# Whole-tile order between readers and writers of PSUM in a recorded program, and one PSUM tile per half for the sums by head

## The chip, the cores and the metric

The kernel runs on one core of one Trainium2 chip. The metric is the device time in microseconds (us) of one execution; the time before is the median of three runs, 963.48 us (959.92 to 965.08).

## The reference

One layer of a hybrid encoder block on 512 tokens of width 1024, in float32. What matters here:

```python
h = rms_norm(x, norm1_g) * (1.0 + sc1) + sh1
xr, yr, q, k, v, gates = jnp.split(h @ w_in, IN_SPLITS, axis=-1)
xr = depthwise_conv(xr, conv_rnn_w, conv_rnn_b, RNN_CONV_LEFT)
# two gates for each of two directions, then two scans
r = sigmoid(einsum('bsnk,dnkj->dbsnj', xb, w_a) + b_a)
i = sigmoid(einsum('bsnk,dnkj->dbsnj', xb, w_i) + b_i)
log_a = -8.0 * r * softplus(-lam)
u = sqrt(-expm1(2.0 * log_a)) * (i * xc)
branch_a = ((h_fwd + h_bwd) * gelu(yr)) @ w_rnn_o
# differential attention, then an RMS norm over each head
o = rms_norm(o, subln_g) * (1.0 - lam_init)
branch_b = o @ w_attn_o
x = x + g1 * ((sigmoid(gate_A) * branch_a + sigmoid(gate_B) * branch_b) @ w_out)
x = x + g2 * (convffn(rms_norm(x, norm2_g) * (1.0 + sc2) + sh2) @ w_down)
return rms_norm(x, final_g)
```

## The kernel before, in words

**Recording and planning.** The kernel's Python code does not issue its instructions at once. A `Recorder` for each engine adds a node to a `Program` (`instruction`, line 203), and `use` (line 182) finds the nodes that it has to come after: a reader comes after the writes that overlap its area of the tile, a writer after the overlapping writes and reads. An area is a box of partitions and columns, so two parts of one tile that do not overlap put no order on each other. Besides, every matmul comes after the last matmul into the same bank (512 columns) of its tile, and a new tile in a buffer comes after all uses of the tile before it.

At the end `order` (line 248) runs through the nodes as a list planner. Each engine has a clock of its own; whenever it is free, it takes the earliest recorded node that is able to run. `cost` (line 226) sets the prices, in a unit of the planner's own: a matmul in FP32R costs its columns plus 32 (544 for 512 columns), one in FP32 four times its columns plus 300 (1324 for 256), a ScalarE activation of 512 columns from PSUM 1581, a new activation table 3080 more. What a matmul releases on another engine is able 360 later. ScalarE ranks a node that needs another table 100 places lower (`PATIENCE`, line 71), but takes it if nothing else is able. The instructions are then emitted in the order of the planned starts, and the tile framework adds the semaphores that this order and the tiles ask for. So the planner decides each engine's queue, and which of two instructions on one tile stands first; how long anything takes on the chip is not its to decide.

**The stages that the change touches.** In the order of time:

- First norm (lines 1019 to 1081): the sum of squares of 512 tokens stands in one PSUM tile `ss1`, written in two halves of 256 columns by FP32 matmuls. ScalarE takes the inverse root of each half into `rstd` (line 1040), then splits the first weight block (`whi`, line 1041); VectorE refines the roots (`newton`, line 635).
- Input convolution: `xrw` is a PSUM tile of two banks for two blocks of 128 channels; `conv_rnn` (line 775) reads each bank by itself.
- Gates (`gates`, line 1143): for each of 8 blocks and 2 directions a PSUM tile `pri` of two banks, [128, 2, 512]. Three matmuls fill bank 0, then three bank 1; then the task `gate` has ScalarE read bank 0 (sigmoid into `r`) and bank 1 (sigmoid into `i`). In between TensorE works through the queue of dense products (`run`, line 583).
- Recurrence (`decays`, `scans`): exponentials, roots and gelus on ScalarE, scans on VectorE.
- Attention: for each head and query block `softmax` (line 1260), four transposes into the tile `pt` (`transposed`, line 1291), two ScalarE copies and two VectorE subtractions that each read half of it, and `product` (line 1316).
- Norm by head: `head_sums` (line 1352) adds 16 matmuls of 256 columns for one half of the tokens into `ssh`, `head_rows` (line 1364) reads that half on ScalarE and VectorE. `ssh` is one tile of two banks, a bank for each half, from the pool `psc` with two buffers; `gates`, `softmax` and `pu` (line 1544) use the same two.
- Output product and second norm: `half` (line 1525) fills the PSUM tiles `op6` and `op7` half by half, and a residual step reads each half.

Of the kernel before, what the change touches and what calls it, by code (L numbers as in the profile page):

```python
# [18 lines left out]
P = 128  # L19
# [3 lines left out]
HEADS = 8  # L23
# [144 lines left out]
class Program:  # L168
# [13 lines left out]
    def use(self, view, write, n, after):  # L182
        t = view.base
        p0, p1, c0, c1 = view.area
        after.add(t.node)

        def meets(u):
            return u[1] < p1 and p0 < u[2] and u[3] < c1 and c0 < u[4]

        after.update(u[0] for u in t.writes if meets(u))  # L190
        if write:
            after.update(u[0] for u in t.reads if meets(u))

            def covered(u):
                return p0 <= u[1] and u[2] <= p1 and c0 <= u[3] and u[4] <= c1

            t.reads = [u for u in t.reads if not covered(u)]
            t.writes = [u for u in t.writes if not covered(u)]
            t.writes.append((n, p0, p1, c0, c1))
        else:  # L200
            t.reads.append((n, p0, p1, c0, c1))

    def instruction(self, engine, owner, name, args, kwargs):
        n, after = len(self.nodes), set()
# [171 lines left out]
def build(nc, tc, ctx, a, out):  # L376
    program = Program(nc)
    V, A, G, T = (
        Recorder(program, e, o) for e, o in ((DVE, nc.vector), (ACT, nc.scalar), (POOL, nc.gpsimd), (PEQ, nc.tensor))
    )  # L380
# [18 lines left out]
    def H(name, dt=F32):  # L399
        n = unused.popleft()  # L400
        t = heap.tile([P, S], dt, tag=f"s{n}", name=name)
        slot_of[id(t)] = n, t
        return t

    def free(*tiles):
        for t in tiles:
            if isinstance(t, (list, tuple)):
                free(*t)
            else:
                unused.append(slot_of.pop(id(t))[0])  # L410
# [14 lines left out]
    def bank2(name):  # L425
        return psc.tile([P, 2, S], F32, tag="sc", name=name)
# [11 lines left out]
    def spawn(gen, delay=0):  # L438
        task = [now[0] + delay, gen]
        tasks.append(task)  # L440
        if not delay:
            advance(task)
# [8 lines left out]
    def until(ready):  # L451

        while not ready():
            assert tasks
            tick()
# [13 lines left out]
    def load(src, n):  # L469
        raw = wraw.tile([P, n], F32, tag="raw", name=f"raw{fetched[0]}")  # L470
        sync.dma_start(raw, src)
        return raw
# [110 lines left out]
    def run(n):  # L583

        while n > 0 and finished[0] < limit[0]:
            r = next(st)
            n -= r
            owed[0] += r
            while owed[0] >= 3:
                owed[0] -= 3  # L590
                tick()
# [6 lines left out]
    for k in range(NK):  # L598
        t = H(f"x{k}")
# [4 lines left out]
    def v(name, j=0, n=1):  # L604
        return vec[:, VEC[name][0] + j : VEC[name][0] + j + n]
# [24 lines left out]
    def inverse_rms(ss, n, r, q):  # L630

        A.activation(r, ss, AF.Abs_reciprocal_sqrt, scale=1.0 / n)
        newton(ss, n, r, q)

    def newton(ss, n, r, q):
        V.tensor_tensor(q, r, r, mult)
        V.scalar_tensor_tensor(q, q, -0.5 / n, ss, mult, mult)
        V.scalar_tensor_tensor(r, q, 1.5, r, add, mult)
# [365 lines left out]
    w = load(a["w_xr"][0], 7 * P)  # L1004
# [33 lines left out]
    rstd, q, t = H("rstd1"), H("rstd1q"), H("hf0")  # L1038
# [40 lines left out]
    w = whi, wlo  # L1079
# [8 lines left out]
    for k in range(NK):  # L1088
        parts3 = (0, 0), (1, 0), (0, 1)
        if k + 1 < NK:  # L1090
            n = k + 1
            t = H(f"hf{n}")
# [27 lines left out]
        for n, (i, j, m, f) in enumerate(passes):  # L1120
            T.matmul(
                xr[m][:, f], w[i][:, m * P : (m + 1) * P], h[k][j][:, f], start=k + i + j == 0 and m == 6,
                stop=k == NK - 1 and i == 0 and j == 1,
# [11 lines left out]
        w = following  # L1135
# [142 lines left out]
    def scores(n, head, qt):  # L1278
        until(lambda: len(qk.get(head, ())) == 3)
        qs, kh, kl = qk[head]  # L1280
        sc = bank2(f"sc{head}{qt}")
        f = slice(qt * P, (qt + 1) * P)
        for c in range(2):
            T.matmul(sc[:, c, :], qs[c][:, f], kh[c], start=True, stop=False)
            T.matmul(sc[:, c, :], qs[c][:, f], kl[c], start=False, stop=True)
        tick()
        spawn(softmax(n, head, qt, sc))
        if qt == 3:
            free(qk.pop(head))
# [26 lines left out]
    def product(head, half):  # L1316
        w = wt.pop((head, half))
        until(lambda: len(w) == 3 and (head // 2, 1) in vs)
        if half == 0:
            po[head] = bank1(f"po{head}", "po")  # L1320
        f = slice(half * 256, half * 256 + 256)
        for k in range(4):
            vv = [b[:, k % 2, (head % 2) * P : (head % 2) * P + P] for _, b in vs[head // 2, k // 2]]
            g = slice((k % 2) * 256, (k % 2) * 256 + 256)
            mm3(po[head][:, f], vv, [t[k // 2][:, g] for t in w[:2]], k == 0, k == 3)
        tick(2)
        free(w[:2])
        if half == 0:
            oT[head] = H(f"oT{head}")
        if half == 1 or head == HEADS - 1:  # L1330
            g = f if head == HEADS - 1 else slice(0, S)
            A.copy(oT[head][:, g], po[head][:, g])
        if half == 1:
            if head % 2 == 1:
                free([[t for t, _ in vs[head // 2, i]] for i in range(2)])
# [4 lines left out]
    def square(j, f):  # L1340
        sq = H(f"osq{j}{f.start}")
        sqs = [H(f"osqs{j}{f.start}{i}", F32R) for i in "hl"]
        A.activation(sq[:, f], oT[j][:, f], AF.Square)
        A.copy(sqs[0][:, f], sq[:, f])
        yield 2
        V.scalar_tensor_tensor(sqs[1][:, f], sq[:, f], EPS, sqs[0][:, f].bitcast(F32), add, sub)
        free(sq)
        for g in HALVES:
            if f.start <= g.start and g.stop <= f.stop:
                squares[j, g.start] = sqs  # L1350

    def head_sums(i, js):
        f = HALVES[i]
        for j in js:
            until(lambda: (j, f.start) in squares)
            sqs = squares[j, f.start]
            for c in range(2):
                w = sel[:, 8 * j : 8 * j + 8]
                T.matmul(ssh[:8, i, :256], w, sqs[c][:, f], start=j + c == 0, stop=j + c == HEADS)
            if i or j == HEADS - 1:  # L1360
                free(sqs)
            run(HS[i])

    def head_rows(i):
        f = HALVES[i]
        inverse_rms(ssh[:8, i, :256], P, rh[:8, f], rhq[:8, f])
        yield 3
        A.copy(rhs[0][:8, f], rh[:8, f])
        yield 1
        V.tensor_tensor(rhs[1][:8, f], rh[:8, f], rhs[0][:8, f].bitcast(F32), sub)  # L1370
        rows.append(i)
# [27 lines left out]
    for n in range(len(steps) + LAG + LAGP):  # L1399
        if n < len(steps):  # L1400
            scores(n, *steps[n])
        if n == len(steps) - 2:
            gsub = keep.tile([P, 1], F32, name="gsub")
            V.tensor_scalar(gsub, v("subln_g"), 1.0 - LAM_INIT, None, mult)
            sel = H("sel", F32R)
            A.copy(sel[:, : HEADS * HEADS], con[:, CS : CS + HEADS * HEADS])
            selb, selr = [H(f"selb{i}", F32R) for i in range(2)], [H(f"selr{i}") for i in range(2)]
            for i in range(2):
                sync.dma_start(selr[i], a["selb"][:, i * S : i * S + S])
            rh, rhq = H("rh"), H("rhq")  # L1410
            rhs = [H("rhh", F32R), H("rhl", F32R)]
            for t in rhs:
                G.memset(t.bitcast(F32), 0.0)
        if n == len(steps):
            for i in range(2):
                A.copy(selb[i], selr[i])
            free(selr)
            for j in range(HEADS - 1):
                if j >= SQ[0]:
                    spawn(square(j, slice(0, S)), 1 + 3 * (j - SQ[0]))  # L1420
        run(STEP[0] + STEPH[2 * (n // 4)] if n < len(steps) else LAST[2 * (n - len(steps))])
        if 0 <= n - LAG < len(steps):
            transposed(n - LAG, *steps[n - LAG])
        if 0 <= n - LAG - LAGP and steps[n - LAG - LAGP][1] % 2 == 1:
            head, qt = steps[n - LAG - LAGP]
            product(head, qt // 2)
            if head == HEADS - 1:
                spawn(square(head, HALVES[qt // 2]), 1)
            elif head < SQ[0] and qt == 3:
                spawn(square(head, slice(0, S)), SQ[1])  # L1430
        if n == len(steps) + 2:
            ssh = bank2("ssh")
            head_sums(0, heads[: HEADS - HL])
            run(HR[0])
            head_sums(0, heads[HEADS - HL :])
            spawn(head_rows(0))
        run(STEP[1] + STEPH[2 * (n // 4) + 1] if n < len(steps) else LAST[2 * (n - len(steps)) + 1])
# [134 lines left out]
    for i, f in enumerate(HALVES):  # L1572
        for k in range(NF):
            if k // 8 == len(wd):
                wd.append(block())
            w = [t[:, (k % 8) * P : (k % 8) * P + P] for t in wd[k // 8]]
# [95 lines left out]
```

## Time and profile before

| what | us |
|---|---|
| median of three runs | 963.48 |
| lowest and highest run | 959.92, 965.08 |
| the profiled execution, its own time | 959.9 |
| its span, first to last instruction | 957.9 |
| TensorE (PE) busy | 925.5 (97%) |
| VectorE (DVE) busy | 660.9 (69%) |
| ScalarE (ACT) busy | 529.4 (55%) |
| GpSimd (POOL) busy | 206.0 (22%) |
| mean granted TensorE clock, share of full speed | 0.988 |

The profiled execution is the fastest of the runs shown; 2.0 us of its time lie outside the span. Busy shares are means over stages of different kinds, so what counts is which engine waits, when, and for whom.

### The profile page before, as it was taken

How to read it: one execution, taken by the hardware profiler on the slowest of the kernel's cores; microseconds unless marked ns; L12 is line 12 of the kernel's file. 1: busy time of each engine (PE TensorE's matmuls, PEld its weight loads, DVE VectorE, ACT ScalarE, POOL GpSimd, SP SyncE). 2: the span in 40 equal slices, each digit the busy share in tenths (PEclk: the TensorE clock that was granted, in tenths of full speed). 3: DMA queues.
4: the chain of work that ended last, by engine and by line, in shares of the span. 5: the costliest groups of instructions: out<-in, count | busy, mean ns of one | idle time of the engine just before them, and what ended most of it. 6: DMA issues, size and time to landing. Idle time of an engine off the chain costs nothing. (4 is left out here: it accounts for less than half of the span.)

```text
span 957.9 us, 12347 instructions
## 1 busy us (share of the span) xinstructions
PE 925.5 (97%) x4596; PEld 779.5 (81%) x4596; DVE 660.9 (69%) x978; ACT 529.4 (55%) x842; POOL 206.0 (22%) x154
## 2 busy tenths in 40 slices
PE   7989999998999999999999999999999999999996
PEld 5777788886879889898778789888888888888885
DVE  6989888998889798778787647566555455422324
ACT  7457999951557667769863326444444444332221
POOL 3000000022355654531142231331111111100101
PEclk8999999999999999999999999999999999999998
DMA  9943232138833233235455440044323323233302
GB/s 341 325 142 120 78 100 66 66 111 269 274 116 89 67 89 111 65 101 168 144 194 166 132 154 23 23 155 132 100 99 93 104 89 92 90 105 98 92 9 88
DMA packets 40051, 116.83 MB, mean 122 GB/s; under 512 B 5816, under 2 KB 8120, under 8 KB 39992
## 3 DMA queue, kind: packets, MB, share of 16 engines
q1 hardware_dynamic: 37120, 114.31, 37.0%
q10 hardware_dynamic: 2872, 1.74, 0.6%
q8 instruction: 36, 0.59, 0.3%
q14 instruction: 23, 0.19, 0.1%
HBM read 109.61 MB, written 2.23 MB: 117 GB/s over the span
## 5 line engine op out<-in xcount | busy, mean ns | idle before, releaser
L221 ACT CAST whi<-raw 128x1024 fp32r<-128x1024 f32 (+1 forms) x135 | 139.2, 1033 | 183.5 <-PE up L221 55.4
L221 DVE TENSOR_TENSOR wlo<-raw,whi 128x1024 fp32r<-128x1024 f32 (+2 forms) x115 | 141.3, 1229 | 122.6 <-PE dn L221 46.2
L221 POOL TENSOR_TENSOR wlo<-raw,whi 128x1024 fp32r<-128x1024 f32 x28 | 70.3, 2513 | 135.8 <-ACT whi L221 65.7
L221 DVE SCALAR_TENSOR_TENSOR fc<-up,vec,fc 128x511 f32<-128x511 f32 x88 | 65.4, 746 | 11.2 <-ACT fc L221 9.7
L221 POOL TENSOR_TENSOR fc<-fc,fc 128x512 f32<-128x512 f32 x22 | 28.5, 1295 | 195.6 <-ACT fc L221 195.6
L221 POOL TENSOR_TENSOR rs<-rs,sinT 128x512 f32<-128x512 f32 x16 | 23.5, 1470 | 209.4 <-PE pk L221 185.5
L221 ACT ACT_TABLE_LOAD x41 | 52.6, 1283 | 5.7 <-DVE fc L221 1.7
L221 DVE SCALAR_TENSOR_TENSOR raw<-raw,crow 128x1024 f32<-128x1024 f32 x32 | 42.0, 1320 | 9.9 <-DMA raw<-in_w_ada 9.7
L221 ACT ACTIVATE p<-sc,mx 128x512 f32<-128x512 f32 x64 | 43.4, 684 | 8.6 <-DVE mx L221 8.3
L221 ACT ACTIVATE fc<-up,vec 128x512 f32<-128x512 f32 x44 | 34.1, 779 | 22.4 <-PE up L221 22.4
L221 DVE TENSOR_REDUCE mx<-sc 128x2 f32<-128x1024 f32 x32 | 39.0, 1217 | 4.0 <-PE sc L221 3.5
L221 ACT ACTIVATE ss<-xx 128x512 f32<-128x512 f32 (+1 forms) x19 | 10.7, 564 | 50.1 <-DVE xx L221 50.1
L221 DVE SCALAR_TENSOR_TENSOR p<-p,sm,p 128x512 f32<-128x512 f32 x32 | 36.7, 1148 | 1.9 <-ACT p L221 1.8
L221 ACT ACTIVATE fc<-fc 128x512 f32<-128x512 f32 x22 | 13.9, 632 | 42.9 <-DVE fc L221 42.8
L221 POOL TENSOR_TENSOR ss<-ss,ss 128x512 f32<-128x512 f32 x8 | 10.6, 1324 | 97.6 <-ACT ss L221 97.6
L221 ACT CAST wth<-pt 128x256 fp32r<-128x256 f32 x64 | 21.1, 377 | 18.4 <-PE pt L221 18.2
L221 DVE TENSOR_TENSOR wtl<-pt,wth 128x256 fp32r<-128x256 f32 x64 | 24.3, 414 | 4.5 <-PE po L221 2.4
L221 PE MATMUL sc<-kh,qs 128*128 128x512 f32 x64 | 24.8, 396 | 1.8 <-DVE qs L221 1.6
L221 ACT ACTIVATE p<-p,sm 128x512 f32<-128x512 f32 x32 | 23.3, 730 | 5.0 <-DVE sm L221 5.0
L221 PE MATMUL sc<-kl,qs 128*128 128x512 f32 x64 | 24.8, 394 | 0.0
L221 DVE TENSOR_TENSOR_SCAN r<-dec,i 128x512 f32<-128x512 f32 x16 | 19.6, 1223 | 0.4
L221 PE MATMUL pt<-con,p 128*128 128x128 f32 x128 | 19.5, 272 | 0.0
(1487 smaller groups left out, 3051.1 us busy)
## 6 DMA issues: line engine op xcount, KB each, us to landing
raw<-in_w_up SPq DMA_DIRECT2D x40, 512.0 KB, 3.3
raw<-in_w_ada SPq DMA_DIRECT2D x32, 512.0 KB, 3.4
raw<-in_w_down SPq DMA_DIRECT2D x16, 512.0 KB, 3.5
rows<-in_w_ada SPq DMA_DIRECT2D x14, 512.0 KB, 7.4
raw<-in_w_ga SPq DMA_DIRECT2D x8, 512.0 KB, 3.3
raw<-in_w_yr SPq DMA_DIRECT2D x8, 512.0 KB, 3.5
raw<-in_w_v SPq DMA_DIRECT2D x8, 512.0 KB, 3.8
raw<-in_w_q SPq DMA_DIRECT2D x8, 512.0 KB, 4.2
```

The lines of the kernel that those rows point to most:

```text
L221: getattr(owner, name)(*map(real, args), **{k: real(b) for k, b in kwargs.items()})
```

## The change

A node in the list of a tile's writes and reads now says which of the two it is. For a tile in PSUM, a reader meets every earlier write and a writer every earlier read, whatever their areas; two writes still meet by their areas, and two reads not at all. Tiles in SBUF keep the old rule. `ssh` becomes two tiles, one for each half, each with the shape of the old one and bank 0 of it in use, so both buffers of `psc` are taken.

```diff
         def meets(u):
-            return u[1] < p1 and p0 < u[2] and u[3] < c1 and c0 < u[4]
+
+            whole = t.psum and u[5] != write
+            return whole or u[1] < p1 and p0 < u[2] and u[3] < c1 and c0 < u[4]
...
-            t.writes.append((n, p0, p1, c0, c1))
+            t.writes.append((n, p0, p1, c0, c1, True))
         else:
-            t.reads.append((n, p0, p1, c0, c1))
+            t.reads.append((n, p0, p1, c0, c1, False))
...
-                T.matmul(ssh[:8, i, :256], w, sqs[c][:, f], start=j + c == 0, stop=j + c == HEADS)
+                T.matmul(ssh[i][:8, 0, :256], w, sqs[c][:, f], start=j + c == 0, stop=j + c == HEADS)
...
-        inverse_rms(ssh[:8, i, :256], P, rh[:8, f], rhq[:8, f])
+        inverse_rms(ssh[i][:8, 0, :256], P, rh[:8, f], rhq[:8, f])
...
-            ssh = bank2("ssh")
+            ssh = [bank2(f"ssh{i}") for i in range(2)]
```

No instruction is added or taken out.

## Rows read from the trace of the kernel before

**Rows 1.** Busy time by stretch: us; PE, PEld, DVE, ACT, POOL; clock; DMA.

```profile
77.00:180.00 103.00, 99.89 (x481) 83.23 (x481) 91.59 (x123) 93.95 (x132) 0.00 (x0) 1.00 0.28 89
...
260.00:480.00 220.00, 217.72 (x1266) 189.01 (x1265) 180.98 (x301) 159.70 (x327) 97.40 (x58) 1.00 0.36 109
```

**Rows 2.** Waits of PE, whole span: waiter, releaser, us in total, times, longest.

```profile
PE pri L221 <- ACT r L221: 3.1, 4, 0.8
...
PE ro L221 <- DVE wlo L221: 2.7, 1, 2.7
...
PE ssh L221 <- DVE rhq L221: 0.5, 1, 0.5
```

**Rows 3.** PE in order of time, first gate: start, us, instruction [idle before, releaser].

```profile
79.10 0.39 PE L221 MATMUL pri<-xs0h,gw0l 128*128 128x512 f32 x1
79.33 0.39 PE L221 MATMUL pri<-xs0l,gw0h 128*128 128x512 f32 x1
80.49 0.50 PE L221 MATMUL pri<-xs0h,gw0l 128*128 128x512 f32 x1 [0.78 <-ACT r L221]
80.83 0.40 PE L221 MATMUL yr<-h1h,whi 128*128 128x512 f32 x1
```

**Rows 4.** ACT in order of time, gates of the first two blocks.

```profile
79.75 0.69 ACT L221 ACTIVATE r<-pri,vec 128x512 f32<-128x512 f32 x1 [0.66 <-PE pri L221]
81.03 0.69 ACT L221 ACTIVATE i<-pri,vec 128x512 f32<-128x512 f32 x1 [0.59 <-PE pri L221]
...
92.20 0.69 ACT L221 ACTIVATE r<-pri,vec 128x512 f32<-128x512 f32 x1 [1.13 <-PE pri L221]
...
94.06 0.61 ACT L221 CAST xs3h<-xc 128x512 fp32r<-128x512 f32 x1
```

**Rows 5.** PE in order of time, sums by head, at the second half's first matmuls.

```profile
475.20 0.28 PE L221 MATMUL ssh<-osqs00h,sel 128*8 128x256 f32 x1
475.99 0.28 PE L221 MATMUL ssh<-osqs00l,sel 128*8 128x256 f32 x1 [0.50 <-DVE rhq L221]
476.10 0.28 PE L221 MATMUL ssh<-osqs10h,sel 128*8 128x256 f32 x1
```

**Rows 6.** Waits of ACT from 76 to 212 us.

```profile
ACT r L221 <- PE pri L221: 5.1, 8, 1.1
...
ACT i L221 <- PE pri L221: 2.4, 4, 0.6
```

**Rows 7.** Waits of DVE from 76 to 212 us.

```profile
DVE gl L221 <- PE yr L221: 3.1, 3, 1.8
...
DVE th L221 <- ACT r L221: 1.5, 4, 0.7
```

**Rows 8.** Busy time by stretch, end of the recurrence.

```profile
207.00:220.00 13.00, 10.41 (x46) 8.27 (x45) 13.00 (x16) 2.41 (x4) 8.78 (x6) 1.00 0.37 121
```

**Rows 9.** ACT in order of time, first norm.

```profile
14.89 0.38 ACT L221 ACTIVATE rstd<-ss 128x256 f32<-128x256 f32 x1 [2.60 <-PE ss L221]
15.17 0.93 ACT L221 CAST whi<-raw 128x896 fp32r<-128x896 f32 x1
16.30 0.38 ACT L221 ACTIVATE rstd<-ss 128x256 f32<-128x256 f32 x1 [0.20 <-DVE rstd1q L221]
```

**Rows 10.** SP's DMA issues in order of time: start, us, transfer.

```profile
8.10 0.43 SPq L221 DMA_DIRECT2D raw<-in_w_xr  x1
```

**Rows 11.** DMA issues from 8.00 to 8.55 us: transfer, count, KB, us to landing.

```profile
raw<-in_w_xr SPq DMA_DIRECT2D x1, 448.0 KB, 6.4
```

**Rows 12.** DVE in order of time, first norm.

```profile
15.30 0.43 DVE L221 TENSOR_TENSOR rstd1q<-rstd 128x256 f32<-128x256 f32 x1 [1.00 <-ACT rstd L221]
...
19.48 0.48 DVE L221 SCALAR_TENSOR_TENSOR h0l<-hf,mod,h0h 128x256 fp32r<-128x256 f32 x1 [0.26 <-ACT h0h L221]
```

**Rows 13.** Who ended the idle time before instructions on the tile pt: us, times.

```profile
  PE pt L221: 18.2, 11
```

**Rows 14.** Groups by cost, from the page: count | busy, mean ns | idle before, releaser.

```profile
L221 ACT ACT_TABLE_LOAD x41 | 52.6, 1283 | 5.7 <-DVE fc L221 1.7
```

## The prediction

> **What bounds the kernel now.** I read the busy time by stretch first. In the gates and the recurrence (77 to 180 us) PE, ACT and DVE are all close to full: 99.89, 93.95 and 91.59 of 103 us. In the attention (260 to 480 us) PE is busy 217.72 of 220 us and the others have room [rows 1]. So a gain has to be idle time of PE, and in the first of these stages it only lasts if ACT and DVE come forward too.
>
> Next I read the list of PE's waits. Two kinds are the change's to remove: a `pri` matmul waits for ACT's `r` four times, 3.1 us in all, and an `ssh` matmul once for DVE's `rhq`, 0.5 us [rows 2]. In the order of time the reader sees what they are. PE has written the fifth of six matmuls into `pri` at 79.33 and starts the sixth at 80.49, after 0.78 us of idleness that ended with ACT's `r` [rows 3]. That `r` reads bank 0, the sixth matmul writes bank 1. It was emitted between the two, so the running program keeps the two in order although they touch different banks. ACT pays as well: `r` waits for the fifth matmul, and `i`, which needs the sixth, waits 0.59 us more behind it [rows 4]. The same shape stands in `ssh`: the second half's first matmul at 475.20, the next at 475.99 behind DVE's read of the first half [rows 5]. So the emitted order makes a wait of which the planner knew nothing.
>
> **The change part by part.** The planner's prices serve here for the order alone; times are those of rows.
>
> *The four stalls in `pri`.* With the new rule `r` is able only after all six matmuls, so it is emitted behind the sixth, and nothing makes PE wait. At the pace of the fourth and fifth (79.10 and 79.33, so 0.23 us a matmul, 0.46 for two) the `yr` matmul that ran at 80.83 would run at 79.33 + 0.46 = 79.79: 1.04 us a stall [rows 3], 4 x 1.04 = 4.2 us for PE [rows 2]. On ACT, the sixth matmul would start at 79.56 and end at 79.95; `r` follows at 79.98 instead of 79.75, `i` 0.59 later at 80.57 instead of 81.03: 0.46 us a stall, 1.8 us for the four [rows 4]. But ACT also sits idle ahead of `r`, eight times for 5.1 us, and ahead of `i`, four times for 2.4 us, each time for PE's `pri` [rows 6]; those come forward with PE. DVE has waits on both that can give way: 3.1 us for PE's `yr` and 1.5 us for ACT's `r` [rows 7]. The stage as a whole thus moves by 1.8 us if only ACT's own saving counts, by 4.2 us if PE's does. I take 3.5, near the upper end, because ACT's idle time lies ahead of the very gates that PE delays.
>
> *Where that stall goes.* What is late next is DVE. From 207 to 220 us it is full (13.00 of 13 us) [rows 8], and PE waits 2.7 us for its `wlo` [rows 2]. If DVE moves with the stage, the 3.5 us pass; if not, this wait grows by what PE gained. The waits of DVE above, each on an engine that comes forward, speak for the first.
>
> *What ACT does in the gaps.* Where `r` becomes able later, ACT's plan has a gap and takes what else is able. At the second block this is likely the copy `xs3h`, which now runs at 94.06 right behind `i` [rows 4] and needs only the convolution: it fits into the 1.13 us that ACT waits at 92.20. That costs nothing, as ACT's own idle time covers it; without that cover it would push `r` back by its 0.61 us. A copy needs no table, so it ranks ahead of the next exponential.
>
> *`ssh`.* With a tile per half nothing orders the second half's matmuls behind the reads of the first. At the pace of the following ones (0.11 us, 475.99 to 476.10) the next would start at 475.31 instead of 475.99: 0.7 us for PE [rows 5]. The second buffer that it takes is free by then: the last scores are read before. Its next user is `pu`, far behind. No other cost.
>
> *First norm.* Here the rule adds a wait. The first half's `rstd` is now able only after the second half's matmuls, 1324 of the planner's units later. On the chip it starts at 14.89, released by the last `ss` matmul, so nothing is lost by that alone. But the copy `whi` now stands between the two `rstd` [rows 9], so it became able about when the first was running; with the later `rstd` the planner may put `whi` first. Its block was issued at 8.10 and took 6.4 us, so it is there at 14.5 [rows 10, 11]. `whi` would run from about 14.55 to 15.48, and `rstd` start at 15.5 instead of 14.89: 0.6 us later, and behind it the first refinement on DVE, which waits for exactly this [rows 12]. Everything of the first norm is queued behind it on DVE. Bounds: 0.2 us less than now if both `rstd` come first (DVE's 0.26 us wait for `h0h` goes [rows 12]), and 0.9 more if `whi` takes its full 0.93. I take +0.6, which follows from the landing.
>
> *`pt`, `xrw`, `op6` and `op7`.* ACT's first copy from `pt` is able after four transposes instead of two. ACT already waits for the transposes, 18.2 us in eleven waits on this tile [rows 13], and PE never waits for these copies; PE's list has no such row. The product that needs them comes a step later. I take nothing, with 1 us either way for changed places in the queues. For `op6` and `op7` a read of one half is long done when the other is written, and `xrw` is read at the end of its stage: nothing.
>
> *The sum.* -3.5 - 0.7 + 0.6 = -3.6 us. On the profiled execution 959.9 - 3.6 = 956.3; that execution is the fastest of the runs shown, 3.6 below the median, so for the median I say 963.48 - 3.6 = 959.9.
>
> **A rule against it.** The trace shows an order between banks of one tile, four times 0.78 us [rows 2, 3]. The Trainium skill, "PSUM — Partial Sum Buffer", section on bank collisions, asks to guard PSUM by bank and quadrant, not by address, so two banks of one tile need no order at all. If the program's waits went by that rule, the change would only hold `r` back; the trace disagrees, so I give this little.
>
> **The rivals.**
>
> *Given back at the end of the recurrence.* DVE's chain up to `wlo` stays where it is, and PE's wait there grows by the 3.5 us. For it: DVE full over 13 us [rows 8]. Against it: DVE's own waits before [rows 7]. Left are -0.7 + 0.6 = -0.1: 963.4 us.
>
> *Slower: tables.* In the gaps before `r` the planner finds nothing without a new table, takes the exponential of an earlier gate and comes back for the sigmoid: two table loads more, 2 x 1.283 = 2.57 us of ACT [rows 14] in the stage where ACT has 9 of 103 us to spare [rows 1]. It decides from the second such detour on (5.1 against 3.6); three give 963.48 - 3.6 + 7.7 = 967.6 us. Against it: the copies that stand ready, as `xs3h`. The Trainium skill, "ScalarE: Activation LUTs", "What ACT_TABLE_LOAD costs", puts a switch at about 2.66 us with a drain, so by it one detour would be an estimated 5.3 us. The row disagrees: all 41 loads have 5.7 us of idle time ahead of them in total [rows 14], no drain for each.
>
> *More.* The new queues also lose the 2.7 us wait for `wlo` [rows 2]: -6.3, 957.2 us.
>
> *No effect.* The waits are not due to the emitted order, or the new order brings them back elsewhere: about 963.5 us, plus 0.6 from the first norm, 964.1.
>
> **How the numbers follow.** Forecast 0.53 (958.4 to 962 on its own), given back 0.17, tables 0.12, more 0.13, no effect 0.05. About 0.5%, 4.8 us here, is what a measurement can tell from no change: faster means under 958.7, slower over 968.3. The forecast's upper end (4.2 + 0.7 + 0.2 = 5.1 us) and "more" lie beyond the lower bound, and the runs shown spread by 5 us: faster 0.32. Tables, with three detours or more, and spread: slower 0.10. The rest is 0.58. The range goes from 955.0 (a little below "more", for the 1 us of the queues and spread) to 967.0 (two detours, 965.0, and the same).
>
> **What would show it.** In the changed kernel's list of waits: no row of PE `pri` on ACT `r`, none of PE `ssh` on DVE `rhq`; `r` and `i` back to back, 0.6 us apart, at all 16 gates; the first `rstd` near 15.5 with `whi` ahead of it. PE's wait for `wlo` should stay near 2.7 us and come 3 us earlier; at 6 us the gain was given back there. The count of table loads should stay at 41; more of them would speak for the slower rival. The prediction is wrong if DVE does not come forward by 190 us, or if changed queues make waits that no row of now shows.

## The result and the profile after

The changed kernel takes 950.2 us in the median of four runs (948.66 to 951.43), where the kernel before takes 964.04 on the same chip: a ratio of 0.9866, 95% interval 0.984 to 0.9893, so 10 to 15 us less. I had forecast 959.9 and a range down to 955.0. The profiled execution took 951.16 us (span 949.2) against 959.9 (span 957.9) before. Two executions of the experiments, one of x1 (1566.41 us) and one of x7 (1326.69 us), ran at a mean granted clock of 0.576 and 0.653; they are left out of the times, and no duration is read from x1's profile, which shows the first of them.

Busy time by stretch of the changed kernel, columns as in [rows 1]; the third line is the end of the recurrence, 4 us earlier than in [rows 8]:

```profile
77.00:180.00 103.00, 103.00 (x502) 87.23 (x501) 96.00 (x130) 97.25 (x136) 0.00 (x0) 1.00 0.28 90
260.00:480.00 220.00, 218.27 (x1274) 189.71 (x1273) 183.05 (x311) 161.84 (x333) 92.88 (x58) 1.00 0.35 108
203.00:216.00 13.00, 10.30 (x47) 8.20 (x45) 13.00 (x16) 2.43 (x5) 8.94 (x6) 1.00 0.36 121
```

PE (TensorE) is now busy for the whole of the gates (103.00 of 103, before 99.89), and DVE (VectorE) and ACT (ScalarE) are busier with it. PE's waits, whole span, columns as in [rows 2]:

```profile
PE xrw L223 <- ACT h0h L223: 3.3, 1, 3.3
PE ro L223 <- DVE wlo L223: 2.7, 1, 2.7
...
PE ss L223 <- DVE sq L223: 1.3, 1, 1.3
...
PE ao L223 <- POOL on1l L223: 0.4, 1, 0.4
```

Both kinds of wait that the change aims at are gone: no `pri` on `r`, no `ssh` on `rhq`. Two more are gone that I had not read in the list of before: `up` on ACT's `fc` (0.9 us, once) and `rb` on DVE's `oT` (1.6 us, twice). The wait for `wlo` stayed at 2.7 us and comes 4.2 us earlier, at 213 to 216 us. Some waits only moved: `xrw` on `h0h` takes 3.3 us in place of 1.4, and `lamps` on `mod`, which stands ahead of it in PE's queue, 0.5 in place of 2.4, so 3.8 for the two in both kernels. `ss` on `sq` grew from 0.6 us to 1.3, and the 0.4 us of `ao` are now for `on1l` in place of `on0h`.

The first gate in order of time, PE and then ACT, as in [rows 3, 4]:

```profile
79.35 0.39 PE L223 MATMUL pri<-xs0h,gw0l 128*128 128x512 f32 x1
79.58 0.39 PE L223 MATMUL pri<-xs0l,gw0h 128*128 128x512 f32 x1
79.81 0.39 PE L223 MATMUL pri<-xs0h,gw0l 128*128 128x512 f32 x1
80.03 0.39 PE L223 MATMUL yr<-h1h,whi 128*128 128x512 f32 x1
```

```profile
80.23 0.69 ACT L223 ACTIVATE r<-pri,vec 128x512 f32<-128x512 f32 x1 [0.80 <-PE pri L223]
80.82 0.68 ACT L223 ACTIVATE i<-pri,vec 128x512 f32<-128x512 f32 x1
...
90.10 0.62 ACT L223 CAST xs3h<-xc 128x512 fp32r<-128x512 f32 x1
91.56 0.69 ACT L223 ACTIVATE r<-pri,vec 128x512 f32<-128x512 f32 x1 [0.84 <-PE pri L223]
```

The matmuls follow each other at 0.23 us with no wait, `r` and `i` stand 0.59 us apart (at 14 of the 16 gates 0.57 to 0.59; at the other two, 1.09 and 1.48 us apart, a copy `ya1h` or `ya2h` stands between them), and at the second block the copy `xs3h` now runs ahead of `r`.

**Where the 13 us are.** I took the start of the same PE instructions in every profile of this study. The stages in between, in us (they are cut at the first `pri`, the first `ro`, the first `rb`, the first `op` on `mg7h`, and the first and the last `up`; the kernels x2 to x12 are described below):

| kernel | start to `pri` | `pri` to `ro` | `ro` to `rb` | `rb` to `op` | `op` to `up` | `up` to last `up` |
|---|---|---|---|---|---|---|
| before | 77.28 | 130.90 | 269.40 | 63.08 | 42.63 | 242.72 |
| after | 77.54 | 126.48 | 269.23 | 59.84 | 42.64 | 241.59 |
| x3 pri | 77.82 | 126.48 | 269.57 | 65.43 | 42.63 | 242.71 |
| x4 up | 79.29 | 130.90 | 269.89 | 64.70 | 42.63 | 241.59 |
| x6 pri, up, ssh | 78.57 | 126.48 | 268.97 | 67.19 | 42.62 | 241.59 |
| x2 rule, one ssh | 77.25 | 126.48 | 269.06 | 59.87 | 42.65 | 241.59 |
| x5 all but ss1 | 81.23 | 126.48 | 268.89 | 59.82 | 42.62 | 241.58 |
| x7 pt, ssh | 78.22 | 130.90 | 268.82 | 59.82 | 42.65 | 242.71 |
| x8 all but pt | 78.53 | 126.48 | 268.35 | 63.34 | 42.64 | 241.59 |
| x9 ss1 | 80.22 | 130.86 | 268.74 | 63.33 | 42.62 | 242.71 |
| x10 row first | 76.98 | 130.86 | 269.95 | 60.13 | 42.64 | 242.72 |
| x11 after again | 75.44 | 126.48 | 268.96 | 59.96 | 42.64 | 241.58 |
| x12 start alone | 76.75 | 130.86 | 268.51 | 63.03 | 42.64 | 242.71 |

Three columns take only two values or two groups of values. The gates (130.9 or 126.5) go with the rule for `pri`, `up` (242.7 or 241.6) with the rule for `pu`, and the norm by head (63.0 to 67.2, or 59.8 to 60.1) with the rule for `pt`, or with the order that x10 adds in its place. The start scatters, 75.4 to 81.2. The profile of before alone would give 959.9 - 951.16 = 8.7 us: its norm by head, 63.08, lies at the low end of the seven profiles with the old order, whose mean is 64.3.

### The profile page after: what moved, and what is told of

Same layout as the page of the kernel before. It is cut to its first block, busy times and chain, and to the rows that moved or that the text cites. A ratio compares the mean times of both kernels' runs of the same rounds, so it can differ in the third digit from the quotient of the medians.

```text
span 949.2 us, 12345 instructions
## 1 busy us (share of the span) xinstructions
PE 922.6 (97%) x4596; PEld 779.2 (82%) x4596; DVE 658.0 (69%) x978; ACT 528.1 (56%) x842; POOL 201.2 (21%) x154
## 5 line engine op out<-in xcount | busy, mean ns | idle before, releaser
L223 DVE SCALAR_TENSOR_TENSOR raw<-raw,crow 128x1024 f32<-128x1024 f32 x32 | 44.7, 1405 | 15.1 <-DMA raw<-in_w_ada 14.9
L223 DVE SCALAR_TENSOR_TENSOR p<-p,sm,p 128x512 f32<-128x512 f32 x32 | 33.6, 1050 | 0.9 <-ACT p L223 0.8
```

Source lines behind the costliest of these rows:

```text
L223: getattr(owner, name)(*map(real, args), **{k: real(b) for k, b in kwargs.items()})
```

## The experiments

Each ratio is to the kernel before, run on the same chip in the same hour; gains in us below are these ratios applied to its time.

| kernel | median us | ratio | 95% interval |
|---|---|---|---|
| x1 ssh tiles alone | 963.35 | 0.9997 | 0.997 to 1.0025 |
| x3 pri | 958.0 | 0.9942 | 0.9922 to 0.9961 |
| x4 up | 961.7 | 0.998 | 0.9963 to 0.9997 |
| x6 pri, up, ssh | 957.91 | 0.9937 | 0.9916 to 0.9958 |
| x2 rule, one ssh | 949.94 | 0.9869 | 0.9831 to 0.9907 |
| x5 all but ss1 | 953.69 | 0.9908 | 0.9877 to 0.9938 |
| x7 pt, ssh | 957.3 | 0.9952 | 0.9928 to 0.9977 |
| x8 all but pt | 954.46 | 0.9909 | 0.988 to 0.9938 |
| x9 ss1 | 962.80 | 0.9996 | 0.9978 to 1.0014 |
| x10 row first | 958.01 | 0.9947 | 0.9927 to 0.9966 |
| x11 after again | 950.98 | 0.9885 | 0.986 to 0.991 |
| x12 start alone | 960.41 | 0.9976 | 0.9955 to 0.9996 |

**x1, a tile `ssh` per half alone**, with the old rule.

```diff
-            ssh = bank2("ssh")
+            ssh = [bank2(f"ssh{i}") for i in range(2)]
```

> A tile per half for the sums by head, with the old rule in the recorded program; every engine's queue stays as it was, only the wait between the halves goes. Theory 'one stall' (the prediction's): the PE ssh wait goes, 0.7 us less, ratio 0.999, and the waits behind it (rb on oT 1.6 us, ao on on0h 0.4 us) stay. Theory 'stall and its followers': the rb and ao waits and the stretch at the lower clock behind them go too, 2.5 to 3.3 us less, ratio 0.997. Theory 'new queues': nothing beyond the ssh wait itself; the rest of the gain in this stage needs the reordering of the full change.

Measured 963.35 us, no difference that can be told: the interval goes from 2.9 us less to 2.4 more, so a gain of 0.7 us can be neither shown nor excluded by these times. The queues are those of before, so the 0.5 us wait for `rhq` [rows 5] is the only thing removed. What that gives is read from x12 below, which has two tiles `ssh` as well, and in this stretch the same PE queue as before:

```profile
474.39 0.28 PE L223 MATMUL ssh<-osqs00h,sel 128*8 128x256 f32 x1
474.51 0.28 PE L223 MATMUL ssh<-osqs00l,sel 128*8 128x256 f32 x1
```

The second half's products follow at once. From the first product on `ssh` to the first on `rb` PE needs 10.3 us in before, x3, x4 and x9, and 9.65 in x6, x8 and x12, whose two tiles are the only difference there: 0.66 us. It lasts: up to the first `op`, before and x9 need 73.4 and 73.6 us, x12 and x8 72.7 and 73.0.

**x3, the rule for `pri` alone.** A flag on each tile says where the rule holds; the other selections below change its line alone.

```diff
-            whole = t.psum and u[5] != write
+            whole = t.whole and u[5] != write
...
+        t.whole = self.psum and name.startswith("pri")
```

> The new rule for the gate tiles pri alone, one ssh tile. Theory 'stalls': the four waits on r go and the stage between the first gate and the first wo product gets 4.2 to 4.4 us shorter, ratio 0.9955. Theory 'given back at the end of the recurrence': the wait of ro on wlo grows from 2.7 to about 6 us and the ratio is 1.000.

Measured 958.0 us, 5.6 below before. The stage from the first `pri` to the first `ro` is 126.48 us in place of 130.90: 4.42, and the wait for `wlo` is still 2.7 us. Nothing is given back.

**x4, the rule for `pu` alone** (`tag == "sc" and name.startswith("up")`).

> The new rule for the two-bank tiles of the first up products alone. The wait of PE up on ACT fc (0.87 us, missed by the prediction) goes: 1.1 us less, ratio 0.999. If that wait was not from this order, it stays and the time is the same.

Measured 961.7 us, 1.9 below. In the profile the stage of `up` is 1.13 us shorter. PE in order of time, the kernel before and then the changed one:

```profile
606.52 0.28 PE L221 MATMUL up<-h27l,wu11h 128*128 128x256 f32 x1
607.67 0.39 PE L221 MATMUL up<-h27h,wu11l 128*128 128x256 f32 x1 [0.87 <-ACT fc L221]
```

```profile
598.96 0.28 PE L223 MATMUL up<-h27l,wu11h 128*128 128x256 f32 x1
599.08 0.28 PE L223 MATMUL up<-h27h,wu11l 128*128 128x256 f32 x1
```

The same shape as in `pri`: a read of one bank was emitted between two matmuls on the other, once in the kernel.

**x6, `pri` and `up` with two `ssh` tiles** (`name.startswith(("pri", "up"))` and the edit of x1): all the waits of PE that a read of the other bank had made.

> The new rule for pri and for the first up products, and a tile per half for the sums; first norm, pt, xrw and the rest keep the old rule. Theory 'stalls': the three places carry the whole gain, so it is at least as fast as the full change, ratio 0.986 to 0.988. Theory 'new queues': the reordering elsewhere carries about half of it, ratio 0.992 to 0.994. Theory 'sum of the three spans' (4.4, 0.7 to 3.3 and 1.1 us): 6 to 9 us of span, ratio 0.991 to 0.9935; what is missing to the full change's 0.9866 would then have to come from the other tiles or from the clock.

Measured 957.91 us, 6 below. So half of the gain does not come from these waits at all; it must come from queues that the rule reorders elsewhere (theory "new queues"). The stage of the norm by head was no shorter here but longer, 67.19 us, and its profile shows two things that the new order could mend. DVE, and the PE matmul that waits for it:

```profile
475.39 1.23 DVE L223 SCALAR_TENSOR_TENSOR raw<-raw,crow 128x1024 f32<-128x1024 f32 x1 [2.35 <-DMA raw<-in_w_ada]
...
476.54 0.41 DVE L223 TENSOR_TENSOR rhl<-rh,rhh 8x256 fp32r<-8x256 f32 x1
```

```profile
477.00 0.50 PE L223 MATMUL rb<-rhl,selb 128*128 128x256 f32 x2 [1.89 <-DVE rhl L223]
```

A reduction of 128 weight rows (`raw`, column 39 of the modulation) is queued between the inverse root and `rhl`. It waits 2.35 us for its DMA, `rhl` waits behind it, and PE for `rhl`. In the profiled execution of before the same reduction stands in the same place, at 476.31, but its rows had landed and it waited for nothing.

Why they had landed there and not here lies one reduction earlier, at DVE and POOL (GpSimd). First the kernel before, then x6, both engines in order of time:

```profile
471.13 1.23 DVE L221 SCALAR_TENSOR_TENSOR raw<-raw,crow 128x1024 f32<-128x1024 f32 x1
471.23 3.39 POOL L221 TENSOR_TENSOR wlo<-raw,whi 128x1024 fp32r<-128x1024 f32 x1 [20.78 <-ACT whi L221]
```

```profile
468.33 2.40 POOL L223 TENSOR_TENSOR wlo<-raw,whi 128x1024 fp32r<-128x1024 f32 x1 [20.79 <-ACT whi L223]
468.42 3.39 DVE L223 SCALAR_TENSOR_TENSOR raw<-raw,crow 128x1024 f32<-128x1024 f32 x1 [0.31 <-DMA raw<-in_w_ada]
```

The two start within 0.2 us of each other in all seven profiles with this order, and the one that starts second takes longer. In before, x8, x9 and x12 DVE is first; its reduction takes 1.2 us, and POOL's `wlo` 3.3 to 3.4. In x3, x4 and x6 POOL is first, by 0.02 to 0.12 us; `wlo` takes 2.4, and the reduction 3.4 to 3.5. The transfer for column 39 is issued right behind that reduction, at 471.85 in x6, so it lands later, and the next reduction waits 2.1 to 2.35 us. These three kernels ran on one chip; whether the chip or chance decides who is first is not shown.

**x2, the rule everywhere, one tile `ssh`** (the edit of x1 left out of the change).

> The rule of the change for every PSUM tile, but one tile ssh for both halves of the norm by head, as before. It tells what the second tile is worth once the rule holds: with one tile every matmul of the second half's sums waits until the first half's inverse root has read. If the tile per half only undoes a wait that the rule itself would make, this kernel gives 951 to 953 us against 950.2 for the whole change, with a wait of PE for rhq of 0.5 to 2 us near 472 in the trace. If the tile per half carries a gain of its own, it gives 954 or more.

Measured 949.94 us, as the whole change, with no wait for `rhq`. Both expectations missed: the planner, told that the second half has to wait for the read of the first, puts three dense products in between. Once the rule holds, the tile per half has no part in the gain that can be measured.

**x5, all but `ss1`** (`name != "ss1"`), **x7, `pt` alone with two `ssh`** and **x8, all but `pt`**, together with x2 in one set.

> The whole change, but the sums of the first norm (ss1) keep the old rule. Three parts that were tried alone and together (pri, up, ssh) gave 6 of the 13 us. Theory A: the rest comes from the new order of the queues that the rule for pt brings in scores and norm by head; then this kernel stands at 949 to 951 us, as the whole change does, since the lateness of the first norm is taken up before 77 us in both. Theory B: the rest comes from the first norm and the clock after it; then it stands at 956 to 958. Stage of the norm by head (from sc at 407 to the first op): 130 us by A, 135 or more by B.

> The rule for the tiles pt alone (transposes of the softmax; it changes places in the queues of PE, DVE, ACT and SP from 290 us on), with a tile ssh per half; all other PSUM tiles by the old rule. Theory A (the order that pt brings is what gives the other half): 955.5 to 958 us, the stage of the norm by head near 130 us, and no wait of PE on rb for rhl. Theory B (first norm): 962 to 964, and that stage at 133 to 137 us. Theory C (the stage needs the rule for ssh and pt together with the shorter gates, because of where the weights then land): 960 to 962.

> The whole change, but the tiles pt keep the old rule. Theory A: 956 to 958 us, the time of the kernel with pri, up and ssh alone (957.9), with the stage of the norm by head at 135 to 137 us and PE waiting for rhl by 1 to 2 us. Theory B: 950 to 952, as the whole change. Theory C: 957 too, but its counterpart, pt alone, then gives little.

x7 takes 957.3 us: `pt` is worth 4.6 us by itself (2.2 to 6.9 by the interval). Its norm by head is 59.82 us, and PE waits neither for `rhl` nor for `oT`. x8, without `pt`, has the old norm by head, 63.34, and takes 954.46, some 4 more than x2, which behaves as the whole change, in the same set. So the rule for `pt` is the larger part of what x6 lacked (theory A), though x5 misses A: at 953.69 it lies 3.8 over x2 in the same set. So something that hangs on `ss1` gains as well. In the two profiles it lies ahead of the first gate: the first `pri` comes at 81.23 us in x5 and at 77.25 in x2, and no other column of the table differs by more than 0.2.

**x10, the old rule with one added order.** If it is the place of the reduction that counts, the gain must come without any rule for PSUM (`LATE` is 39):

```diff
+        if f == LATE:
+            program.after[-1].add(program.row)
...
         V.tensor_tensor(rhs[1][:8, f], rh[:8, f], rhs[0][:8, f].bitcast(F32), sub)
+        if not i:
+            program.row = len(program.nodes) - 1
```

> The kernel before, old rule and one tile ssh, with one added order: the modulation of the weight rows of column 39 (the step on DVE that waits for its DMA) comes after the row rhl of the first half of the norm by head. Planned so, the second half's rb products also come ahead of the last gb products, as under the rule for pt, with no PSUM order touched. Theory A (the place of one modulation ahead of rhl and the late rb products are what the rule for pt removes): the time falls by what pt gave, 4 to 6 us, to 957.5 to 959.5, the stretch from the first rb to the first ao is 9.7 to 10.5 us in place of 11.4 to 14.8, and the clock stays whole between 470 and 500 us. Theory B (the gain of pt sits in the scores or in the transposes themselves): 962.5 to 964.5, with the stretch as before.

Measured 958.01 us, 0.9947: what `pt` gave. The first `ao` follows the first `rb` after 10.35 us, and the clock is 1.00 from 470 to 500 us, both as theory A asked. DVE now has the row ahead of the reduction:

```profile
476.98 0.41 DVE L222 TENSOR_TENSOR rhl<-rh,rhh 8x256 fp32r<-8x256 f32 x1 [0.19 <-ACT rhh L222]
477.32 1.21 DVE L222 SCALAR_TENSOR_TENSOR raw<-raw,crow 128x1024 f32<-128x1024 f32 x1
```

From there the planner goes on much as under the rule for `pt`: more of the `rb` products come ahead of the last `gb` products. Without that they stand behind them and PE runs dry. So x10 shows that the gain needs no rule for PSUM; it does not part the place of the reduction from the new order of `rb` that follows from it. The kernel before, PE:

```profile
488.05 0.39 PE L221 MATMUL rb<-rhh,selb 128*128 128x256 f32 x1 [0.33 <-DVE oT L221]
...
488.95 0.50 PE L221 MATMUL ao<-on0h,whi 128*128 128x512 f32 x1 [0.39 <-ACT on0h L221]
490.68 0.58 PE L221 MATMUL rb<-rhh,selb 128*128 128x256 f32 x1 [1.23 <-DVE oT L221]
...
491.27 0.68 PE L221 MATMUL ao<-on0l,whi 128*128 128x512 f32 x1
491.75 0.63 PE L221 MATMUL ao<-on1h,whi 128*128 128x512 f32 x1
```

and the changed kernel at the same work:

```profile
482.92 0.40 PE L223 MATMUL ao<-on0h,whi 128*128 128x512 f32 x1
483.43 0.39 PE L223 MATMUL rb<-rhh,selb 128*128 128x256 f32 x1
483.66 0.28 PE L223 MATMUL rb<-rhl,selb 128*128 128x256 f32 x1
483.77 0.49 PE L223 MATMUL ao<-on0l,whi 128*128 128x512 f32 x1
484.10 0.40 PE L223 MATMUL ao<-on1h,whi 128*128 128x512 f32 x1
```

In the first, three waits of 0.33, 0.39 and 1.23 us stand close together, and after them an `ao` product takes 0.63 to 0.68 us in place of 0.40. The granted clock of that stretch goes with it: busy time by stretch, before, then changed, then x10.

```profile
489.00:494.00 5.00, 3.77 (x12) 3.07 (x13) 4.49 (x9) 2.32 (x6) 2.64 (x4) 0.67 0.82 279
```

```profile
483.00:488.00 5.00, 4.42 (x22) 3.16 (x21) 4.45 (x10) 3.91 (x11) 4.23 (x3) 1.00 0.81 257
```

```profile
488.00:493.00 5.00, 4.01 (x21) 3.04 (x20) 4.75 (x9) 3.85 (x10) 4.64 (x4) 1.00 0.62 202
```

TensorE fell from its full clock, 2.4 GHz, to the lower level, 1.2 GHz, after the waits; a mean of 0.67 means most of the stretch at the lower one. As an estimate, 3.77 us busy at 0.67 is 3.77 x 0.33 = 1.2 us lost, on top of the 1.95 us of waits: together 3.2, against one wait of 0.4 us in the changed kernel, so 2.8. The table's 63.08 - 59.84 = 3.24 holds besides 0.6 us for three products that the new order puts ahead of the first `rb`; without them it is 2.7, near the estimate. In x6 the wait for `rhl` brings a fall of its own, ahead of this one:

```profile
476.00:482.00 6.00, 5.00 (x19) 4.13 (x20) 5.38 (x15) 2.85 (x6) 0.73 (x1) 0.72 0.27 94
```

The Trainium skill, "TensorE: Matmul & The Clock Gate", section "HAM oscillation — how this bites in real kernels", says of a kernel that waits for a DMA after each batch of matmuls that these waits send the array back to the low clock, so that the next batch starts slow. These rows agree in kind, with shorter waits (0.33 to 1.23 us) and other engines to wait for. By them the price of the waits in this place is an estimated 3.2 / 1.95 = 1.6 times their length. Not every wait has that price: behind a single wait of 0.99 us for the same products in x10, and of 1.23 in x2, the clock stayed at 1.00, and so it did in the kernel before behind 1.70 us for `h4h` (43 to 50 us) and 1.58 for `qs` (281 to 291 us).

**x9, the rule for `ss1` alone** (`name == "ss1"`), **and x11, the changed kernel again**, run with x10.

> The rule for the sums of the first norm (ss1) alone, all else as before: on ACT the rounding whi of the first weights goes ahead of both rstd, on DVE wlo and two small steps go ahead of the Newton steps, on PE one group of three products changes places; nothing moves after 25 us. Two comparisons price it: the whole change against all but ss1 (950.1 against 953.7) and all but pt against pri, up and ssh alone (954.5 against 957.9). Theory A: it is a gain of its own, 3.5 us, and this kernel stands at 959.5 to 961 us where the kernel before stands at 963.6; the gain shows as a start in which TensorE's clock doesn't fall at 57 to 62 us. Theory B (the recorded prediction): the first weights' rounding costs 0.6 us and later waits take it up, 963.5 to 964.2. Theory C: the comparisons differ by what else they carry and the price is between, 961.5 to 963.

> The changed kernel once more, on the chip and in the hour of the two kernels above. Theory A of the clock: the start of this kernel (first product of the first gate at 77 to 78 us) has no fall of the clock at 57 to 62 us in this profile either. Theory C: the fall comes and goes by chance, the first gate then starts at 78.5 to 81 us, and the kernel's times spread by as much as those of the kernel before. Median 949 to 951.5 by both.

x9 is no faster, 0.9996 (2.1 us less at most), so `ss1` by itself does not give the 3.5 us of theory A (its 962.80 us lie in the numbers of theory C, but the kernel before stood at 962.33 in this set, not at 963.6). x11 repeats the gain, 950.98 us. The queues of x9 and of the changed kernel differ in the start by a few places of DVE and ACT alone, all due to the other tiles read there.

**x12, the start alone**: all tiles but `pri`, `up` and `pt`. Up to 80 us its queues are those of the changed kernel, behind that those of before.

> The rule for all PSUM tiles but pri, up and pt, with a tile ssh per half: up to 80 us the queues are those of the whole change, behind that those of the kernel before. Against the kernel with the rule for ss1 alone the start differs by two places on DVE: the step red (for the rotary lines) stands in the first norm's gap, not at 34 us, and one reduction of weight rows (rows15) comes ahead of other work, by which h5 follows h4 after 3.8 to 3.9 us, not 5.1. Theory A: those two places carry what ss1 alone didn't give: 959 to 961 us where the kernel before stands at 962.5 to 963.8, h5 3.8 to 3.9 us behind h4, first gate some 55 to 57 us behind the first product on h0 (58 to 60 with the old start). Theory B: the 3.5 us between the whole change and all but ss1 need the later parts too, or came by chance: 962.5 to 964.

Measured 960.41 us, 0.9976: 2.3 us from the new order of the start, with an interval from 0.4 to 4.3. ACT in order of time in x12, and DVE at that moment:

```profile
42.44 0.72 ACT L223 ACTIVATE h4h<-hf,mod 128x512 fp32r<-128x512 f32 x1
46.23 0.72 ACT L223 ACTIVATE h5h<-hf,mod 128x512 fp32r<-128x512 f32 x1 [3.08 <-DVE mod L223]
```

```profile
41.16 1.22 DVE L223 SCALAR_TENSOR_TENSOR rows<-rows,crow 128x1024 f32<-128x1024 f32 x1
...
43.19 0.75 DVE L223 SCALAR_TENSOR_TENSOR h4l<-hf,mod,h4h 128x512 fp32r<-128x512 f32 x1 [0.80 <-ACT h4h L223]
...
44.77 1.22 DVE L223 SCALAR_TENSOR_TENSOR rows<-rows,crow 128x1024 f32<-128x1024 f32 x1
```

The same two views of x9:

```profile
44.37 0.72 ACT L223 ACTIVATE h4h<-hf,mod 128x512 fp32r<-128x512 f32 x1
49.43 0.72 ACT L223 ACTIVATE h5h<-hf,mod 128x512 fp32r<-128x512 f32 x1 [4.34 <-DVE mod L223]
```

```profile
45.12 0.75 DVE L223 SCALAR_TENSOR_TENSOR h4l<-hf,mod,h4h 128x512 fp32r<-128x512 f32 x1 [0.63 <-ACT h4h L223]
45.79 1.22 DVE L223 SCALAR_TENSOR_TENSOR rows<-rows,crow 128x1024 f32<-128x1024 f32 x1
...
47.97 1.22 DVE L223 SCALAR_TENSOR_TENSOR rows<-rows,crow 128x1024 f32<-128x1024 f32 x1
```

In x12 one of the two row reductions between `h4l` and `h5` stands ahead of `h4l`, so `h5` has one less in front of it; it follows `h4` after 3.79 us in place of 5.06 (4.10 in the changed kernel). PE's wait for `h6h`, two blocks on, is 2.1 to 2.6 us in the five profiles with this order and 2.7 to 3.5 in the eight others. From the first product on `h0h` to the first gate the five profiles with this order need 55.0, 55.0, 55.2, 56.8 and 57.0 us, the eight with another 57.8 to 60.2.

## Why the prediction was wrong, step by step

The direction and the mechanism of the four stalls were right; the size of the whole was not: 13 us against 3.6. By its own steps:

- **The stalls in `pri`: mis-sized, -3.5 against -4.4.** The stage moved by 4.42 us in every kernel with the rule for `pri`, the upper bound (4.2) and a little more. I took less for fear that ACT's own saving of 1.8 us would hold the rest, and ACT's idle time gave way instead: ahead of `r` it went down from 5.1 us [rows 6] to 3.9, and the 2.4 us ahead of `i` are gone (its waits from 76 to 212 us, after):

```profile
ACT r L223 <- PE pri L223: 3.9, 6, 0.8
```

- **Where that stall goes: right.** DVE came forward with the stage; the wait for `wlo` is 2.7 us as before, 4.2 us earlier. The rival "given back" and the rival "more" are both out.
- **What ACT does in the gaps: right.** `xs3h` ahead of `r` at no cost. The sign "at all 16 gates" held at 14; at the two others the planner put a copy between `r` and `i`, not a table load. There are 41 table loads as before [rows 14], so the slower rival is out (page of after, groups by cost):

```profile
L223 ACT ACT_TABLE_LOAD x41 | 52.6, 1283 | 5.1 <-DVE fc L223 1.8
```

- **`ssh`: right by the profiles, -0.7 against -0.66 (x12, under x1).** The times of x1 cannot tell so little from nothing. What I had not seen is that the rule alone removes the stall too (x2): the second tile isn't needed for it. In the table the 0.66 us lie in the column from `ro` to `rb`, where the three products that the new order moves ahead of the first `rb` (0.58 us) hide them.
- **First norm: the step that was named happened, but did not reach the first gate.** `whi` does run ahead of both `rstd`:

```profile
14.41 0.94 ACT L223 CAST whi<-raw 128x896 fp32r<-128x896 f32 x1 [2.02 <-DMA raw<-in_w_xr]
17.58 0.66 ACT L223 ACTIVATE rstd<-ss 128x256 f32<-128x256 f32 x2 [2.23 <-PE ss L223]
```

  `rstd` waits for the sums, which came later than in the profile of before (14.89, [rows 9]), in the main because PE ran them at the lower clock (two products of 512 columns in 2.05 us, 1.10 before). In x12, at full clock up to 16 us as in before, `rstd` starts at 14.83 right behind `whi`, and the first product on `h0h` at 19.78, in place of 19.50 in before and 19.14 in x10: 0.3 to 0.6 us later, so the size up to there was about right. Over all executions that product starts at 21.3 us in the mean of the five profiles with the new start, 20.1 in the seven with the old. But I followed the queues only up to there. Behind it, DVE's row reductions moved, and the first gate comes no later (77.1 us in the mean of the five, 78.5 of the seven); x12 gains 2.3 us.
- **`pt`: the step that failed.** "I take nothing, with 1 us either way for changed places in the queues." I asked who waits for the reads of `pt`, found no one, and stopped. The rule moves those reads by a step, and with them every queue up to the end of the norm by head. That was worth 4 to 5 us (x7, x8, x10), as much as the four stalls in `pri` together, in place of nothing: the waits for `oT` and `on0h`, in some executions that for `rhl`, and the falls of the clock behind them.
- **`pu`: left out, a second term put at nothing.** The row `up` on `fc`, 0.9 us, stood in the same list as [rows 2] and has the same shape as `pri`. I named `pu` only as the next user of a buffer. It gave 1.1 us in the profile, 1.9 in the times (0.3 to 3.6).
- **The profile that I argued from was the fastest execution.** I carried its 3.6 us over to the median as if every stage shared them. It lacked the wait for `rhl` that three of the seven profiles with the old order show (1.4 to 1.9 us), so a part of what the change removes did not stand in its rows. Its norm by head, 63.08 us, is 1.2 below the mean of the seven.

The sum of the stages, with the mean of the profiles for the two that scatter: gates 4.4, norm by head 64.3 - 59.9 = 4.4, `up` 1.1, start 2.3 by the times of x12: 12.2 us, against 10 to 15 measured. The last term is the least certain.

**Left open.** Between 55 and 65 us the clock fell in all ten profiles other than those of the changed kernel, its repetition and x2; in these three it did not. x8 and x12 have the same queues up to 80 us, and fell. Busy time by stretch, the changed kernel and x12:

```profile
56.00:62.00 6.00, 4.33 (x19) 3.59 (x20) 4.24 (x9) 2.76 (x4) 0.00 (x0) 1.00 0.46 135
```

```profile
56.00:62.00 6.00, 6.00 (x21) 4.78 (x21) 5.89 (x11) 2.72 (x3) 0.00 (x0) 0.76 0.22 44
```

The length of PE's wait for `h6h` does not decide it: 2.3 to 2.6 us in the three, 2.1 and 2.3 in the two. With equal queues it may be the moment at which the waits fall in that execution, or chance; three profiles against two do not tell. The first gate comes 55.0 to 55.2 us behind the first product on `h0h` in the three, 56.8 and 57.0 in the two. That may be why x2, with the whole rule, stands 3.8 us below all but `ss1`, while the start alone gives 2.3.

## What to carry to other kernels

When a change touches the order rules of a planner, don't stop at the waits that it removes: list each instruction that changes its place in each queue, and ask of each what it waits for (a DMA above all) and who stands behind it. Price a wait of TensorE with the time at the lower clock that follows it, where the rows show one, and read the list of waits once for the shape of the stall, over all tiles, not for the tiles that the change names. Compare the profiled execution with the median before carrying its waits over: it can lack waits that other executions have. And where a part is too small for the times, as the 0.66 us of `ssh`, cut the profiles at the same two products and compare the stretch.

## What was not expected of the hardware

Short waits that stand close together can bring TensorE's clock down: 0.33, 0.39 and 1.23 us within 3 us of the norm by head were followed by a stretch at a mean of 0.67, with matmuls of 0.63 to 0.68 us in place of 0.40, while longer single waits elsewhere in the same execution (1.58 and 1.70 us) had none. And the same instruction at the same place of its queue can cost nothing or more than 2 us, by whether its DMA has landed: the reduction of column 39 waited 0 us in the profile of before and 2.35 in x6. A start 0.1 us earlier or later decided that: behind POOL's `wlo` the reduction before it took 3.39 us, ahead of it 1.23.
